# Layer norm between the last two attentions of a two-block model, with tokens on partitions

## The chip, the core and the metric

The kernel runs on one core of a Trainium2 chip, in one launch. The metric is the device time in microseconds of one execution. Three runs of the kernel before took 1597.56, 1601.13 and 1601.93 us; the median, 1601.13 us, is its time.

## The reference

The model is a block with a convolution, a dilated window attention and a feed-forward part, followed by a second block of two layers. In the second block each layer is an attention (first one with selected keys, then one with stick-breaking weights), an output projection, a residual and a layer norm. The change touches the layer norm of the first of these two layers, whose result is the input of the second layer's projections.

```python
D_MODEL, SEQ, N_HEADS = 1024, 512, 16
LN_EPS = 1e-5
ALPHA = (2.0 * DEPTH_2) ** 0.25

def layer_norm(x, g, b):
    xf = x.astype(jnp.float32)
    mu = jnp.mean(xf, axis=-1, keepdims=True)
    var = jnp.mean(jnp.square(xf - mu), axis=-1, keepdims=True)
    return ((xf - mu) * lax.rsqrt(var + LN_EPS) * g + b).astype(x.dtype)

def stick_breaking_mixer(x, w_in, w_out):
    q, k, v, g = jnp.split(x @ w_in, 4, axis=-1)
    ...
    return (o * jax.nn.silu(g)) @ w_out

def second_block(x, ...):
    for i in range(DEPTH_2):
        ...                                   # y = attention of layer i
        x = layer_norm(ALPHA * x + y, ln_g[i], ln_b[i])
    return x
```

## The kernel before

All activations lie turned: channels on the 128 partitions, the 512 tokens along the row, so that 1024 channels are 8 blocks of 128x512. A matrix product takes both operands in two parts, a rounded high part and the rest (`Ah`, `Al` of an activation, `whi`, `wlo` of a weight), and adds three matmuls for each of 8 chunks of the contraction (lines 301 to 303): high by high, low by high, high by low.

Weights come in blocks of 512 KB. SyncE's queue loads the raw block (line 87, two buffers), ScalarE rounds it to `whi` (line 119, four buffers), and GpSimd subtracts to get `wlo` (line 123, four pieces of 128x256). A block's raw buffer is free for the next load when GpSimd is through with it, its `whi` buffer when TensorE is.

TensorE runs in the order in which the program is written: a stream of (product, chunk) pairs is pulled, and small pieces of work are put behind a given number of further chunks (`pe.after`). The other engines' orders are laid out by a scheduler from the program's order and readiness.

The stage of the change starts when the attention of the layer is through. `Outward` holds the output projection's 8 products. Of blocks 0 to 3 all chunks but the last have been run before; `run` (line 1213 on) runs those last chunks, then blocks 4 and 5 over all 512 tokens, then blocks 6 and 7 for the first 256 tokens (the first half) and then for the second. `done` (line 1209) adds each block to the residual `e` (the tiles named S) and calls `summed`.

`Between` is the norm in question. Its sums go over channels, that is over partitions, so it makes them on TensorE with matrices of ones. After block 3 it takes half of the channels' mean as a middle (`middle`, line 1237) and subtracts it from every block (line 1249), squares on ScalarE (1252, 1255) and adds squares and values on GpSimd and VectorE (1257 to 1260). For each half `stats` (line 1275) sends the sums, rounded and rest, through four matmuls with ones, takes Ln and Exp for the scale, and goes over all 8 blocks: subtract the mean (1296), multiply by gain and scale (1297), high part on ScalarE (1298), low part on VectorE (1299). `normed` then runs the first three of the next layer's 8 gate products in halves, chunk by chunk for all three together, as the chunks of `Ah` and `Al` appear.

`Last` is the norm at the end of the program. It turns each block with transposes on TensorE (line 1312), copies it to a tile `y` with tokens on partitions, takes statistics along the row on VectorE (1319, 1341), and Ln and Exp for the scales of two row tiles at a time (line 192 is the helper that issues them).

Behind the stage follow the gates' Tanh on ScalarE, the first query and key products of the next layer (lines 530 to 560), and GpSimd's additions of the next residual (line 1204). These stand in a loop over head pairs that lasts to about 1545 us.

Of the kernel before, what the change touches and what calls it, by code (L numbers as in the profile page):

```python
# [10 lines left out]
F32 = mybir.dt.float32  # L11
# [39 lines left out]
STATS = (9, 14)  # L51
# [97 lines left out]
def model_kernel(ctx: ExitStack, tc: tile.TileContext, x, norm1_g, w_in, gate_b, conv_w, conv_b, conv_norm_g,  # L149
# [27 lines left out]
    def f32(t):  # L177
        return t.bitcast(F32)
# [40 lines left out]
    ones_h = const.tile([128, 128], F32R, name="ones_h")  # L219
# [203 lines left out]
    with tc.tile_pool(name="rows", bufs=1) as rows, tc.manual_schedule(engines={  # L423
# [19 lines left out]
        nc.vector.tensor_scalar(ones_h, zero128, 2.0 / D, None, op0=OP.add)  # L443
# [774 lines left out]
    class Between(Outward):  # L1218

        def summed(self, c, ts):
            part = self.part
            if c == 1:
                nc.vector.tensor_add(part, self.es[0], self.es[1])
            elif c in (2, 3):
                nc.vector.tensor_add(part, part, self.es[c])
            if c == 3:
                h, l = act_pair(self.pool, "st", 2)
                nc.scalar.copy(h, part)  # L1230
                nc.vector.tensor_sub(l, part, f32(h))
                pe.after(4, lambda: self.middle(h, l))
            self.ready.append((c, ts))
            if self.centred:
                self.shift(c, ts)

        def middle(self, h, l):
            pm = ps_t()
            nc.tensor.matmul(pm, ones_h, h, start=True, stop=False)
            nc.tensor.matmul(pm, ones_h, l, start=False, stop=True)  # L1240
            nc.scalar.copy(self.mid, pm)
            self.centred = True
            for a in self.ready:
                self.shift(*a)

        def shift(self, c, ts):
            t = slice(*ts)
            es, s1, s2 = [e[:, t] for e in self.es], self.s1[:, t], self.s2[:, t]
            nc.vector.tensor_sub(es[c], es[c], self.mid[:, t])
            eng = nc.gpsimd if c < 4 else nc.vector  # L1250
            if c == 0:
                nc.scalar.activation(s2, es[c], AF.Square)
            else:
                sq = self.pool.tile([128, S], F32, name="sq", bufs=3)[:, t]
                nc.scalar.activation(sq, es[c], AF.Square)
                if c == 5:
                    eng.tensor_add(s1, es[4], es[5])
                elif c > 5:
                    eng.tensor_add(s1, s1, es[c])
                eng.tensor_add(s2, s2, sq)  # L1260
            if c == ND - 1:
                half = TS.index(ts)
                pe.after(STATS[half], lambda: self.stats(half))

        def normed(self, pool, ys, prods):

            self.pool, self.ready, self.centred, self.ys = pool, [], False, ys
            self.mid, self.part, self.s1, self.s2, self.var = (pool.tile([128, S], F32, name=n)
                                                               for n in ("mid", "part", "s1", "s2", "var"))
            self.run()  # L1270
            for half in range(2):
                pe.together(*[p[half] for p in prods])
            pe.finish()

        def stats(self, half):
            t = slice(*TS[half])
            n = S // 2
            p1, p2 = ps_t()[:, :n], ps_t()[:, :n]
            for p, s in ((p1, self.s1), (p2, self.s2)):
                h, l = (a[:, :n] for a in act_pair(self.pool, "st", 2))  # L1280
                nc.scalar.copy(h, s[:, t])
                nc.vector.tensor_sub(l, s[:, t], f32(h))
# [303 lines left out]
```

## Time and profile before

| | |
|---|---|
| median of three runs | 1601.13 us |
| the profiled execution | 1601.03 us |
| its span, first to last instruction | 1598.9 us |
| TensorE busy | 1527.2 us, 96% of the span |
| VectorE, ScalarE, GpSimd busy | 70%, 53%, 50% |
| mean granted clock of TensorE | 0.98 |

A page of a profile gives for each engine the time in which it was busy, in a picture of 40 slices and as groups of instructions by line. PE is TensorE, DVE VectorE, ACT ScalarE, POOL GpSimd, SP SyncE. PEclk is the clock that TensorE was granted as a share of 2.4 GHz: 1.00 is 2.4 and 0.50 is 1.2 GHz, the two levels. A row of the timeline begins with the start and the length of an instruction; what stands in brackets is the idle time of its engine just before it and what ended that.

### The profile page before, as it was taken

To read this page: it belongs to the slowest core of one execution; us is meant where nothing else is said; L and a number is where in the kernel's file an instruction comes from. 1 tells how busy PE (TensorE), PEld (TensorE's weight loads), DVE (VectorE), ACT (ScalarE), POOL (GpSimd) and SP (SyncE) were. 2 spreads that over 40 slices of the span, in tenths; PEclk is the share of its full clock that TensorE was granted. 3 is DMA by queue.
4 is the path that set the end of the run, shared out by engine and by line. 5 is a ranking of instruction groups with operands and counts; after the bars stand their busy time and mean duration, and the time that the engine had idled before them with its cause. 6 is when DMAs were issued, how large, how long until landed. Compare 5 with 4: busy or idle time off the path is not lost.

```text
span 1598.9 us, 21378 instructions
## 1 busy us (share of the span) xinstructions
PE 1527.2 (96%) x7870; PEld 1296.7 (81%) x7870; DVE 1121.4 (70%) x1837; ACT 845.4 (53%) x1524; POOL 806.5 (50%) x680
## 2 busy tenths in 40 slices
PE   7999799998999999999999999999999789999996
PEld 6877688887878888888888887888887678888885
DVE  8998777776166467727735669988887765777764
ACT  4455787777552444424333444366766345666652
POOL 3789944332744653454444474445442875334324
PEclk9999899999999999999999999999999899999998
DMA  4323212221233423343333242322220313212212
GB/s 149 88 87 98 86 54 73 60 67 40 67 105 105 126 86 92 93 118 91 90 110 89 84 125 66 80 80 66 67 67 14 92 40 106 67 54 80 67 52 80
DMA packets 234604, 130.37 MB, mean 82 GB/s; under 512 B 5206, under 2 KB 232774, under 8 KB 234500
## 3 DMA queue, kind: packets, MB, share of 16 engines
q1 hardware_dynamic: 234356, 128.75, 27.7%
q8 instruction: 62, 1.02, 0.3%
q14 instruction: 42, 0.34, 0.1%
q10 hardware_dynamic: 144, 0.26, 0.0%
HBM read 126.90 MB, written 2.10 MB: 81 GB/s over the span
## 4 chain that ended last, share of the span: by engine, by line
PE 57%; DVE 23%; ACT 7%; POOL 5%; issue 5%; DMA 2%; DVEq 0%; SPq 0%; ACTq 0%; POOLq 0%
PE pj L301 10%; PE pj L302 9%; PE pj L303 9%; PE s L302 5%; PE s L303 5%; PE s L301 5%; DVE pt L831 5%; PE o L512 2%; POOL wlo L123 2%; PE pt L593 2%; PE pj L325 2%; PE pj L327 2%; PE pj L326 2%; POOL S L837 2%; DVE score L1442 1%
## 5 line engine op out<-in xcount | busy, mean ns | idle before, releaser
L123 POOL TENSOR_TENSOR wlo<-wraw,whi 128x256 fp32r<-128x256 f32 (+2 forms) x548 | 653.8, 1218 | 684.4 <-ACT whi L119 639.0
L301 PE MATMUL pj<-Ah,whi 128*128 128x512 f32 (+3 forms) x896 | 362.2, 404 | 15.2 <-DVE v L718 9.8
L119 ACT CAST whi<-wraw 128x1024 fp32r<-128x1024 f32 (+3 forms) x255 | 243.8, 965 | 224.3 <-PE pj L302 82.1
L303 PE MATMUL pj<-Ah,wlo 128*128 128x512 f32 (+3 forms) x896 | 350.4, 391 | 2.5 <-POOL wlo L123 2.5
L302 PE MATMUL pj<-Al,whi 128*128 128x512 f32 (+3 forms) x896 | 350.7, 391 | 0.0
L301 PEld LDWEIGHTS pj<-Ah,whi 128*128 128x128 f32 (+1 forms) x896 | 171.2, 191 | 41.9 <-issue 9.1
L303 PEld LDWEIGHTS pj<-Ah,wlo 128*128 128x128 f32 (+1 forms) x896 | 170.3, 190 | 39.1 <-POOL wlo L123 3.4
L302 PEld LDWEIGHTS pj<-Al,whi 128*128 128x128 f32 (+1 forms) x896 | 171.1, 191 | 24.4
L301 PE MATMUL s<-Ah,whi 128*128 128x512 f32 (+1 forms) x352 | 135.8, 386 | 4.0 <-ACT Ah L1298 4.0
L302 PE MATMUL s<-Al,whi 128*128 128x512 f32 (+1 forms) x352 | 135.7, 386 | 3.6 <-DVE Al L1299 3.6
L303 PE MATMUL s<-Ah,wlo 128*128 128x512 f32 (+1 forms) x352 | 135.6, 385 | 1.0 <-POOL wlo L123 1.0
L831 DVE SCALAR_TENSOR_TENSOR pt<-S,cw,pt 128x496 f32<-128x496 f32 (+19 forms) x180 | 124.8, 738 | 6.4 <-ACT pt L824 3.8
L325 PE MATMUL pj<-whi,Ah 128*128 128x256 f32 x384 | 112.4, 293 | 1.4 <-DVE q L533 1.4
L596 DVE TENSOR_TENSOR PTl<-pt,PTh 128x512 fp32r<-128x512 f32 x144 | 86.0, 598 | 32.9 <-ACT PTh L595 31.9
L327 PE MATMUL pj<-whi,Al 128*128 128x256 f32 x384 | 108.4, 282 | 0.0
L326 PE MATMUL pj<-wlo,Ah 128*128 128x256 f32 x384 | 108.3, 282 | 0.0
L192 ACT ACTIVATE P<-P,nm 128x128 f32<-128x128 f32 (+3 forms) x128 | 72.0, 563 | 63.2 <-DVE nm L626 61.9
L744 DVE SCALAR_TENSOR_TENSOR u<-ur,fw,u 128x511 f32<-128x511 f32 x44 | 74.9, 1705 | 37.5 <-ACT u L743 37.5
L837 POOL TENSOR_TENSOR S<-S,o 128x511 f32<-128x511 f32 (+29 forms) x60 | 78.2, 1317 | 15.4 <-ACT o L836 14.3
L595 ACT CAST PTh<-pt 128x512 fp32r<-128x512 f32 x144 | 73.1, 513 | 19.6 <-PE pt L593 19.1
L302 PEld LDWEIGHTS s<-Al,whi 128*128 128x128 f32 x352 | 67.8, 193 | 17.1 <-DVE Al L1299 4.5
L301 PEld LDWEIGHTS s<-Ah,whi 128*128 128x128 f32 x352 | 67.9, 193 | 17.1 <-ACT Ah L1298 4.6
(334 smaller groups left out, 3250.8 us busy)
## 6 DMA issues: line engine op xcount, KB each, us to landing
wraw<-in_w_in_dram SPq DMA_DIRECT2D x56, 512.0 KB
wraw<-in_w_up_dram SPq DMA_DIRECT2D x44, 512.0 KB
wraw<-in_w_in_a_dram SPq DMA_DIRECT2D x36, 512.0 KB
wraw<-in_w_in_b_dram SPq DMA_DIRECT2D x32, 512.0 KB
wraw<-in_w_down_dram SPq DMA_DIRECT2D x16, 512.0 KB
wraw<-in_w_attn_out_dram SPq DMA_DIRECT2D x8, 512.0 KB
wraw<-in_w_conv_out_dram SPq DMA_DIRECT2D x8, 512.0 KB
wraw<-in_w_out_dram SPq DMA_DIRECT2D x8, 512.0 KB
```

What stands on the lines that cost most here:

```text
L119: nc.scalar.copy(h, s)
L123: nc.gpsimd.tensor_sub(l[:, k], s[:, k], h[:, k].bitcast(F32))
L301: nc.tensor.matmul(o, hv[:, k, :], ah, start=first, stop=False)
L302: nc.tensor.matmul(o, hv[:, k, :], al, start=False, stop=False)
L303: nc.tensor.matmul(o, lv[:, k, :], ah, start=False, stop=last)
L325: nc.tensor.matmul(o, ah, hv, start=k == 0, stop=False)
L326: nc.tensor.matmul(o, ah, lv, start=False, stop=False)
L327: nc.tensor.matmul(o, al, hv, start=False, stop=k == 7)
L596: nc.vector.tensor_sub(l[:, :at], pt[:, :at], f32(h)[:, :at])
L744: nc.vector.scalar_tensor_tensor(u[:, 1:], v[:, :S - 1], fw[:, 1, j:j + 1], u[:, 1:], op0=OP.mult, op1=OP.add)
L831: nc.vector.scalar_tensor_tensor(o, a, w, o, op0=OP.mult, op1=OP.add)
L837: nc.gpsimd.tensor_add(o, o, t)
```

## The change

`Between` now works as `Last` does up to the scales. Their common part is the new class `Turned`: each block is turned as soon as it is complete, copied to `y`, and its statistics are taken along rows (`bn_stats`, `bn_aggr`). When a half's last block is turned, `finish` takes the scales of the half's two row tiles, and the mean times the scale, negative (`off`, 128x1). Then the two row tiles of the half are normalised in place, 512 columns at a time, one on VectorE, the other on ScalarE. `back` turns the result again: for each of the 8 blocks two transposes into one PSUM bank, ScalarE's high part with gain and bias per partition, the full value `e` (on ScalarE for odd blocks, on VectorE for even ones), and VectorE's subtraction for the low part. The backs stand 7, 9, 11, ... chunks behind the turning of block 7 (`BACK`). The middle, the squares and the matmuls with ones go, and with them the matrix `ones_h`. `Last` is the same as before, apart from where its lines stand.

```diff
-STATS = (9, 14)
+BACK = (7, 2)
...
-    class Between(Outward):
-        def summed(self, c, ts):
...
-        def middle(self, h, l):
...
-        def shift(self, c, ts):
...
-        def stats(self, half):
...
-    class Last(Outward):
+    class Turned(Outward):
         SPANS = {3: (0, 4), 6: (4, 7), 7: (7, 8)}
         def summed(self, c, ts):
...
             pe.after(4, turn)
+        def buffers(self, pool):
...
+        def scales(self, ts):
+            rstd = self.rstd[:, ts[0]:ts[-1] + 1]
+            for t in ts:
+                nc.vector.bn_aggr(self.mv[:, t], self.stats[:, t])
+            act(rstd, self.mv[:, ts[0]:ts[-1] + 1, 1], AF.Ln, bias=eps5)
+            act(rstd, rstd, AF.Exp, scale=-0.5)
+
+    class Between(Turned):
+        def normed(self, pool, ys, prods):
+            self.buffers(pool)
+            self.off = pool.tile([128, NT], F32, name="off")
+            self.ys = ys
+            self.run()
+            for half in range(2):
+                pe.together(*[p[half] for p in prods])
+            pe.finish()
+
+        def finish(self, ts):
+            self.scales(ts)
+            mv, rstd, off = self.mv, self.rstd, self.off
+            for t in ts:
+                nc.vector.scalar_tensor_tensor(off[:, t:t + 1], mv[:, t, 0:1], -1.0, rstd[:, t:t + 1], op0=OP.mult, op1=OP.mult)
+            for k in range(0, D, 512):
+                for t in ts:
+                    z = self.y[:, t, k:k + 512]
+                    if t % 2:
+                        nc.scalar.activation(z, z, AF.Identity, bias=off[:, t:t + 1], scale=rstd[:, t:t + 1])
+                    else:
+                        nc.vector.tensor_scalar(z, z, mv[:, t, 0:1], rstd[:, t:t + 1], op0=OP.subtract, op1=OP.mult)
+            for c in range(ND):
+                pe.after(BACK[0] + BACK[1] * c, lambda c=c: self.back(c, ts))
+
+        def back(self, c, ts):
+            if ts[0] == 0:
+                self.ys.append(act_pair(keep, "A", ND))
+            pt = ps_t()[:, :S // 2]
+            for i, t in enumerate(ts):
+                nc.tensor.transpose(pt[:, 128 * i:128 * i + 128], self.y[:, t, 128 * c:128 * c + 128], ident)
+            h, l = (a[:, 128 * ts[0]:128 * ts[-1] + 128] for a in self.ys[c])
+            g, b = lng[:, c:c + 1], lnb[:, c:c + 1]
+            e = self.pool.tile([128, S // 2], F32, name="e", bufs=3)
+            nc.scalar.activation(h, pt, AF.Identity, bias=b, scale=g)
+            if c % 2:
+                nc.scalar.activation(e, pt, AF.Identity, bias=b, scale=g)
+            else:
+                nc.vector.tensor_scalar(e, pt, g, b, op0=OP.mult, op1=OP.add)
+            nc.vector.tensor_sub(l, e, f32(h))
+
+    class Last(Turned):
```

On TensorE, where block 7 of the second half (`pj`, over `ogh` and `ogl`, the attention's output) has run its first chunks, before: the four matmuls with ones for the first half's statistics.

```order
L303 MATMUL pj_11393<-ogh_9329,wlo_11243 128x256
L1283 MATMUL pt_11397<-sth_11399,ones_d_72 128x256
L1284 MATMUL pt_11397<-stl_11400,ones_d_72 128x256
L1283 MATMUL pt_11398<-sth_11405,ones_d_72 128x256
L1284 MATMUL pt_11398<-stl_11406,ones_d_72 128x256
L301 MATMUL pj_11393<-ogh_9612,whi_11242 128x256
L302 MATMUL pj_11393<-ogl_9613,whi_11242 128x256
```

And at the place that answers to it, with the change:

```order
L301 MATMUL pj_11404<-ogl_9914,whi_11239 128x256
L302 MATMUL pj_11404<-ogh_9913,wlo_11240 128x256
L1287 MATMUL pt_11416<-ident_69,y_11155 128x128 x2
L300 MATMUL pj_11404<-ogh_10196,whi_11239 128x256
L301 MATMUL pj_11404<-ogl_10197,whi_11239 128x256
L302 MATMUL pj_11404<-ogh_10196,wlo_11240 128x256
L1227 MATMUL pt_11426<-ident_69,S8_10876 128x128 x2
L300 MATMUL pj_11404<-ogh_10499,whi_11239 128x256
```

The matmuls with ones are gone; in their place two transposes of the normalised `y` (L1287) and, a chunk later, the turning of block 6's second half (L1227) stand between the chunks. Line numbers are those of the changed file.

On ScalarE, from the first half's sums on, before (`sth` the rounded sums, `Ah` the high parts, `whi<-wraw` a weight cast):

```order
L1281 CAST sth_11399<-s1_11159 128x256
L1281 CAST sth_11405<-s2_11160 128x256
L119 CAST whi_11491<-wraw_11289 128x1024
L1286 ACTIVATE var_11161<-pt_11397 128x256
L1255 ACTIVATE sq_11389<-S8_10878 128x256
L192 ACTIVATE var_11161<-var_11161,eps5_71 128x256
L192 ACTIVATE var_11161<-var_11161 128x256
L119 CAST whi_11504<-wraw_11329 128x1024
L1298 ACTIVATE Ah_11416<-S8_10686,vec_77 128x256
L1298 ACTIVATE Ah_11422<-S8_10716,vec_77 128x256
```

And from the last copy of the first half on, with the change:

```order
L1228 COPY y_11155<-pt_11375 128x2x128
L192 ACTIVATE rstd_11158<-mv_11157,eps5_71 128x2
L119 CAST whi_11463<-wraw_11287 128x1024
L192 ACTIVATE rstd_11158<-rstd_11158 128x2
L1276 ACTIVATE y_11155<-y_11155,off_11159,rstd_11158 128x512 x2
L1291 ACTIVATE Ah_11414<-pt_11416,vec_76 128x256
L1228 COPY y_11155<-pt_11426 128x2x128
L1291 ACTIVATE Ah_11435<-pt_11437,vec_76 128x256
L1293 ACTIVATE e_11440<-pt_11437,vec_76 128x256
L1291 ACTIVATE Ah_11450<-pt_11452,vec_76 128x256
L119 CAST whi_11485<-wraw_11328 128x1024
```

A weight cast now stands between Ln and Exp of the scales (L192), and the high parts (L1291) and full values (L1293) come from PSUM in turn with the copy of block 6's second half (L1228) and another cast.

## Rows read from the trace of the kernel before

**Rows 1.** Windows: stretch, length, busy us per engine (count), clock, DMA share, GB/s.

```profile
1236.70:1305.90 69.20, 54.49 (x311) 48.60 (x310) 56.37 (x81) 26.52 (x47) 53.24 (x56) 0.85 0.21 61
1245.10:1249.20 4.10, 4.10 (x13) 3.19 (x12) 1.59 (x2) 1.53 (x2) 2.91 (x5) 0.58 0.51 152
1293.30:1296.80 3.50, 3.50 (x17) 3.50 (x18) 3.50 (x4) 0.38 (x2) 3.50 (x3) 0.51 0.02 5
1306.00:1545.00 239.00, 236.60 (x1399) 207.35 (x1398) 165.11 (x258) 151.44 (x303) 103.44 (x130) 1.00 0.25 71
1318.40:1323.00 4.60, 4.59 (x38) 4.60 (x39) 1.13 (x2) 3.60 (x6) 3.04 (x5) 1.00 0.43 118
1559.70:1580.85 21.15, 20.52 (x133) 18.20 (x132) 5.87 (x11) 5.79 (x9) 9.62 (x14) 1.00 0.17 51
```

**Rows 2.** TensorE's waits from 1236.7 to 1305.9: us, times, longest.

```profile
PE pt L1283 <- ACT sth L1281: 5.1, 2, 4.7
...
PE s L301 <- ACT Ah L1298: 4.0, 3, 2.3
...
PE s L302 <- DVE Al L1299: 3.6, 4, 1.5
```

**Rows 3.** Groups by line and shape, 1236 to 1306 us: busy, mean ns, idle.

```profile
L123 POOL TENSOR_TENSOR wlo<-wraw,whi 128x256 fp32r<-128x256 f32 x32 | 30.0, 970 | 8.7 <-ACT whi L119 8.7
...
L1297 DVE SCALAR_TENSOR_TENSOR S<-S,vec,var 128x256 f32<-128x256 f32 x16 | 13.9, 916 | 0.0
```

**Rows 4.** Groups by line and shape, the whole run.

```profile
L743 ACT ACTIVATE u<-ur,fw 128x512 f32<-128x512 f32 x44 | 35.8, 815 | 17.0 <-DVE ur L741 17.0
...
L718 DVE TENSOR_TENSOR v<-pj,v 128x256 fp32r<-128x256 f32 x48 | 20.1, 418 | 12.7 <-ACT v L717 12.5
...
L1157 ACT ACTIVATE ogh<-tmp 128x512 fp32r<-128x512 f32 x16 | 10.1, 632 | 15.0 <-DVE tmp L1155 11.2 <-DVE tmp L1478 3.8
...
L1313 ACT COPY y<-pt 128x256 f32<-128x256 f32 x4 | 1.5, 367 | 7.3 <-PE pt L1312 7.3
```

**Rows 5.** Timeline of TensorE inside the stage: start, length, instruction.

```profile
1257.77 0.28 PE L301 MATMUL s<-ogh,whi 128*128 128x256 f32 x1
...
1260.65 0.28 PE L301 MATMUL pj<-ogh,whi 128*128 128x256 f32 x1
...
1292.13 0.39 PE L301 MATMUL s<-Ah,whi 128*128 128x256 f32 x1 [1.28 <-ACT Ah L1298]
...
1293.24 0.47 PE L302 MATMUL s<-Al,whi 128*128 128x256 f32 x1 [0.73 <-DVE Al L1299]
```

**Rows 6.** Timeline of TensorE and ScalarE in the last norm.

```profile
1556.26 0.39 PE L301 MATMUL pj<-ogh,whi 128*128 128x512 f32 x1
...
1569.78 0.63 PE L1312 MATMUL pt<-ident,e 128*128 128x128 f32 x4 [0.63 <-DVE e L1209]
...
1580.84 0.38 PE L1312 MATMUL pt<-ident,e 128*128 128x128 f32 x2
...
1580.98 0.37 PE L301 MATMUL pj<-ogh,whi 128*128 128x256 f32 x1
...
1581.18 0.29 PE L302 MATMUL pj<-ogl,whi 128*128 128x256 f32 x1
...
1582.46 0.30 ACT L192 ACTIVATE rstd<-mv,eps 128x2 f32<-128x2 f32 x1 [0.83 <-DVE mv L1341]
...
1582.79 0.20 ACT L192 ACTIVATE rstd<-rstd 128x2 f32<-128x2 f32 x1
...
1589.18 0.81 ACT L1352 ACTIVATE y<-y,mr,nr 128x512 f32<-128x512 f32 x1
```

**Rows 7.** Timeline of GpSimd, ScalarE and TensorE just behind the stage.

```profile
1305.65 2.53 POOL L1204 TENSOR_TENSOR e<-Ah,Al 128x512 f32<-128x512 f32 x2
...
1314.69 1.05 ACT L119 CAST whi<-wraw 128x1024 fp32r<-128x1024 f32 x1 [3.08 <-DMA wraw<-in_w_in_b_dram]
...
1318.41 0.36 PE L325 MATMUL pj<-whi,Ah 128*128 128x256 f32 x1 [1.44 <-DVE q L533]
```

More of the change, by code (lines that the diff above doesn't have):

```diff
@@ L218, in model_kernel @@
     ones_d = const.tile([128, 128], F32R, name="ones_d")
-    ones_h = const.tile([128, 128], F32R, name="ones_h")
     ones_b = const.tile([128, 128], F32R, name="ones_b")
@@ L442, in model_kernel @@
         nc.vector.tensor_scalar(ones_d, zero128, 1.0 / D, None, op0=OP.add)
-        nc.vector.tensor_scalar(ones_h, zero128, 2.0 / D, None, op0=OP.add)
         nc.vector.tensor_scalar(ones_b, zero128, 0.0, None, op0=OP.add)
@@ L1216, in run @@
                 pe.skewed(p)
-    class Between(Outward):
-        def summed(self, c, ts):
[L1223 to L1235, printed above, removed]
-        def middle(self, h, l):
[L1238 to L1244, printed above, removed]
-        def shift(self, c, ts):
[L1247 to L1273, printed above, removed]
-        def stats(self, half):
[L1276 to L1282, printed above, removed]
-                nc.tensor.matmul(p, ones_d, h, start=True, stop=False)
-                nc.tensor.matmul(p, ones_d, l, start=False, stop=True)
-            mu, var = self.part[:, t], self.var[:, t]
-            nc.scalar.activation(var, p1, AF.Square)
-            nc.vector.tensor_copy(mu, p1)
-            nc.vector.tensor_sub(var, p2, var)
-            act(var, var, AF.Ln, bias=eps5)
-            act(var, var, AF.Exp, scale=-0.5)
-            for c, e in enumerate(self.es):
-                e, g, b = e[:, t], lng[:, c:c + 1], lnb[:, c:c + 1]
-                if half == 0:
-                    self.ys.append(act_pair(keep, "A", ND))
-                h, l = (a[:, t] for a in self.ys[c])
-                (nc.gpsimd if c > 2 else nc.vector).tensor_sub(e, e, mu)
-                nc.vector.scalar_tensor_tensor(e, e, g, var, op0=OP.mult, op1=OP.mult)
-                nc.scalar.activation(h, e, AF.Identity, bias=b)
-                nc.vector.scalar_tensor_tensor(l, e, b, f32(h), op0=OP.add, op1=OP.subtract)
@@ L1323, in summed @@
             pe.after(4, turn)
-        def normed(self, pool):
+        def buffers(self, pool):
             self.pool = pool
@@ L1331, in normed @@
+    class Last(Turned):
+        def normed(self, pool):
+            self.buffers(pool)
             self.g, self.b = (pool.tile([128, D], F32, name=n) for n in "gb")
@@ L1337, in finish @@
         def finish(self, ts):
-            mv, g, b = self.mv, self.g, self.b
-            rstd = self.rstd[:, ts[0]:ts[-1] + 1]
-            for t in ts:
-                nc.vector.bn_aggr(mv[:, t], self.stats[:, t])
-            act(rstd, mv[:, ts[0]:ts[-1] + 1, 1], AF.Ln, bias=eps5)
-            act(rstd, rstd, AF.Exp, scale=-0.5)
-            rstd = self.rstd
+            self.scales(ts)
+            mv, rstd, g, b = self.mv, self.rstd, self.g, self.b
             for t in ts:
```

## The prediction

> **What bounds the kernel now.** I read first the windows, because an average over the whole span hides the one stage that the change touches. The reader is to see two things in them [rows 1]. The stretch behind the stage (1306 to 1545 us) has TensorE busy for 236.6 of 239 us at the full clock: there a microsecond won or lost earlier is simply moved along. The stage itself, from the first last-chunk matmul of the output projection (1236.70) to the first full-width matmul of the next layer (1305.90), takes 69.2 us, with TensorE busy 54.5 of them at a mean clock of 0.85, while VectorE is busy for 56.4.
>
> Second, the waits of TensorE inside the stage [rows 2]: the three longest groups sum to 5.1 + 4.0 + 3.6 = 12.7 us. All are waits for numbers of the norm: the rounded sums that go into the matmuls with ones, the high parts (Ah), the low parts (Al).
>
> Third, what the engine that it waits for is doing: VectorE's steps at L1297 take 0.916 us on average for 256 columns [rows 3], against 0.418 us for a two-operand step of the same width with one operand in PSUM [rows 4]. GpSimd's subtractions for the weights, in the same stage, take 0.970 us [rows 3].
>
> Fourth, the clock. There are four stretches in the stage at the level of 1.2 GHz; the first (from 1245.1) and the last (from 1293.3) stand in [rows 1]. Each follows waits, the last one waits of 1.28 and 0.73 us [rows 5]. It costs 3.5 x 0.49 = 1.7 us, the first 4.1 x 0.42 = 1.7, four of them some 7 us. So about 20 of the 69 us are waits and what they do to the clock.
>
> **What goes, what comes, and what it costs.** The statistics by matmuls with ones go, with the middle, the squares, the sums, and the passes of VectorE and GpSimd over eight blocks in each half. What comes is the mechanism that the last norm uses already, up to the scales; then two normalising steps of 512 columns for each row tile, 16 pairs of transposes back, and for each block and half one high part, one full value and one low part.
>
> *From the start of the stage to the turning of block 7, first half.* TensorE's order here becomes that of the last norm, instruction for instruction, so I take its time from there: 1556.26 to 1580.84 is 24.6 us [rows 6], which includes a wait of 0.63 us for VectorE at 1569.78. ScalarE has two weight casts more here than there (the first two gate blocks), each waiting for its DMA. They stand ahead of two copies of turned blocks that nothing needs for microseconds; I count them at nothing, and at 1.05 us each [rows 7] if that slack is gone.
>
> *From there to the end, TensorE's own work.* A matmul of 256 columns starts every 0.12 us (24 of them from 1257.77 to 1260.65 [rows 5]), so a group of three takes 0.36. There are 12 groups left of the projection and 48 of the gates: 21.6 us. A pair of transposes takes 0.14 us and delays the start after the next matmul by 0.08 (1580.84, 1580.98, 1581.18 [rows 6]): 0.22. One pair closes the first half, two come from the second half, 16 are the way back: 19 x 0.22 = 4.2 us. Sum 25.8 us.
>
> *Its waits there.* The first pair back stands 0.22 + 7 x 0.36 = 2.7 us behind the turning of block 7. The chain of the scales: Ln ends 1.92 us after that turning [rows 6]; then a weight cast of 1.05 us [rows 7] stands on ScalarE between Ln and Exp; Exp takes 0.20 [rows 6]; two 128x1 steps on VectorE, not seen before, I take at 0.3 together, the Ln's time for as small a tile [rows 6] (between 0, if something hid them, and 0.84, two steps of 256 columns [rows 4]); a normalising step of 512 columns on ScalarE, 0.81 us [rows 6]. That ends at 4.3: a wait of 1.6 us, behind which the last five groups of the projection and the turning of block 6's second half are queued. Then the first block's Ah and Al take their round trip beside those five groups, and I allow 0.4 us for the first Al.
>
> In the second half ScalarE has a queue ahead of the scales: two evacuations in hand, a copy of 0.37, five evacuations, Ln, Exp and the 0.81. An evacuation of 256 columns from PSUM with a bias and a scale per partition does not occur before; its bounds are the plain copy, 0.37 [rows 4], and 0.81, twice the columns with both. I take 0.367 + (0.815 - 0.632) = 0.55, the difference being that of 512 columns with and without the two per-partition operands [rows 4]. Together 5.5 us, against 7 groups and 4 pairs, 3.4 us, on TensorE: 2.1 us of wait, with the gates of the first half from their fourth chunk on queued behind it. After that the gates find everything ready, since a pair back comes every 2 groups and a chunk of the three gates takes 3. Waits together 4.1 us; bounds 0.6 (the first without its cast, the second hidden) and 8.2 (twice as long).
>
> *The clock.* A wait of 1.44 us at 1318.41 [rows 7] left it at 1.00 [rows 1]; 1.28 and 0.73 us close together before 1293.3 did not [rows 5]. My two waits lie around that. I take one low stretch, 1.7 us; bounds none and three.
>
> *VectorE's low parts.* Al is a subtraction of two SBUF tiles while GpSimd may be working on weights. I take 0.42 us, the undisturbed row [rows 4], since GpSimd has weights to do for only part of the stage; the other end is 0.92 [rows 3]. Sixteen times the difference is 8 us on an engine with room beside TensorE's 30, so some 2 us at most reach the end. The Trainium skill (SBUF — State Buffer, section Who interferes with whom) says that a VectorE instruction with two SBUF inputs contends with a GpSimd instruction that reads SBUF, and that one fully blocks the other; by that rule the change keeps 16 such instructions and the sum would be up to 2 us longer. The trace agrees with it: 0.916 against 0.418 us.
>
> *Sum.* New stage 24.6 + 25.8 + 4.1 + 1.7 = 56.2 us, against 69.2: 13.0 us less. GpSimd loses its subtractions and sums for the norm, so its eight additions for the last residual no longer run past the end of the stage: before, they ended at 1308.18, and only then came the next weights, whose successor's DMA ScalarE waited for (3.08 us) and TensorE behind it (1.44 us) [rows 7]. I count 1.2 us of that 1.44 as won, bounds 0 and 1.4. The order of the loads on SP is the same. Total 14.2 us.
>
> The profiled execution took 1601.03 us (a span of 1598.9 and 2.1 around it), next to the median of 1601.13; 1601.0 - 14.2 = 1586.8.
>
> **The rivals.**
> 1. *ScalarE's queue becomes the bound.* Casts that wait for DMA stand in its order between the scales and the evacuations. If the raw block is late by 3.08 us [rows 7] at two of them, 6 us more reach TensorE: 1593. For it: such waits occur before. Against it: the change takes away most of the VectorE steps beside which GpSimd ran slow, so the loads that wait for GpSimd start earlier.
> 2. *The clock stays low from the first wait to the end of the gates.* At the low level a matmul of 256 columns takes 3.5/17 = 0.206 us [rows 1], so 60 groups cost 60 x 3 x 0.086 = 15.5 us more, less the 1.7 counted: 1600.6, no change. For it: two waits and many transposes between short matmuls. Against it: 26 transposes among matmuls ran at 1.00 in the last norm (1559.7 to 1580.85 [rows 1]). The Trainium skill (TensorE: Matmul & The Clock Gate, section Part 4: PE-mode transpose) says that the full clock does not engage for transposes; by that rule this rival would be the likelier, and the trace speaks against its mattering among matmuls.
> 3. *The weights take the gain back.* If the next stage were led by its DMAs, it would wait out the 14 us: 1601. Against it: a DMA share of 0.25 from 1306 to 1545 and TensorE busy for 99% [rows 1].
> 4. *The round trips don't overlap; slower.* Each of the 16 pairs back is followed by 0.38 us of transposes, up to two evacuations of 0.55 and a subtraction of up to 0.92 before the block can be used. If TensorE waited out these 2.4 us at each, that is 38 us in place of the 4.1 counted: 1621. It is slower from 14.2/16 = 0.9 us for each block upwards. Against it: three PSUM banks for turned blocks, two groups between a pair and the next, three between the uses.
>
> **How the numbers follow.** The forecast, 1587 with its own range of 1581 to 1592, has 0.80; rival 1 0.10; rival 2 0.04; rival 3 0.03; rival 4 0.03. A measurement of this kernel can tell about 0.3%, 4.8 us, from no change. Forecast and rival 1 lie below 1596: 0.90 faster. Rivals 2 and 3 make 0.07 for the same, rival 4 0.03 for slower. The range runs from 1580 (no low clock, no wait but the 0.63 us: 14.2 + 1.7 + 4.1 and 0.2 of the queries' wait, rounded) to 1595, past rival 1.
>
> **What would show it.** In the new profile the stretch from the projection's last chunks to the first full-width matmul of the next layer should last 53 to 61 us, TensorE's waits in it sum to 3 to 9 us, with one of 1 to 2.5 us at the first pair back of each half, and at most two low stretches of the clock. VectorE should be busy for about half of it. The 1.44 us wait on the queries behind it should shrink. I am wrong if the stage is over 64 us, if waits of 1 us or more stand at single blocks inside the gates, or if the stage is short and the end is not earlier.

## The result: 1584.0 us in place of 1601.5, and the profile after

| | before | after |
|---|---|---|
| median of runs | 1601.51 us (4 runs, 1597.56 to 1601.93) | 1584.03 us (4 runs, 1582.43 to 1587.29) |
| ratio | | 0.9899, 95% interval 0.9877 to 0.9921 |
| profiled execution, span | 1601.03, 1598.9 us | 1583.91, 1582.1 us |

Predicted were 1586.8 us. A second comparison (after_again, below) gave 0.9909, 0.9897 to 0.9922: by the two medians the change is worth some 14 to 17 us.

Windows of the kernel after, columns as in [rows 1]: the stage, its two parts (up to and from the turning of block 7's first half), the two stretches behind the first wait, the time around the second wait, and what answers to the long stretch behind the stage.

```profile
1233.08:1288.90 55.82, 52.06 (x366) 48.31 (x365) 30.82 (x58) 28.90 (x51) 35.13 (x44) 0.97 0.26 76
1233.08:1257.66 24.58, 23.97 (x147) 20.99 (x146) 8.36 (x14) 9.68 (x13) 16.88 (x24) 1.00 0.38 109
1257.66:1288.90 31.24, 28.09 (x221) 27.32 (x220) 22.46 (x44) 19.22 (x38) 18.25 (x20) 0.95 0.17 50
1262.50:1264.00 1.50, 1.50 (x10) 1.50 (x11) 1.14 (x2) 1.38 (x3) 1.28 (x2) 0.73 0.00 0
1264.00:1267.50 3.50, 3.50 (x22) 3.50 (x21) 2.31 (x7) 2.12 (x5) 0.00 (x0) 0.63 0.54 150
1272.40:1276.00 3.60, 2.42 (x19) 2.24 (x20) 2.65 (x8) 3.40 (x8) 0.00 (x0) 1.00 0.48 150
1288.90:1528.00 239.10, 237.34 (x1401) 207.82 (x1400) 165.59 (x258) 151.99 (x303) 102.42 (x129) 1.00 0.25 71
```

The stage went from 69.20 to 55.82 us, and VectorE's work in it from 56.4 to 30.8 us [rows 1]. The clock is low in one stretch: 1.5 x 0.27 + 3.5 x 0.37 = 1.7 us.

TensorE's waits in the stage (us in total, times, longest), against 14.6 us in eleven waits before, the longest of them in [rows 2]:

```profile
PE pt L1287 <- ACT y L1276: 1.9, 1, 1.9
PE pt L1287 <- DVE y L1278: 1.1, 1, 1.1
PE pt L1227 <- DVE S L1207: 0.6, 1, 0.6
```

The timeline of ScalarE, VectorE and TensorE between the first half's scales and the first pair back, and TensorE at the second half's first pair:

```profile
1259.29 0.30 ACT L192 ACTIVATE rstd<-mv,eps 128x2 f32<-128x2 f32 x1 [0.83 <-DVE mv L1250]
1259.52 1.05 ACT L119 CAST whi<-wraw 128x1024 fp32r<-128x1024 f32 x1
1260.47 0.20 ACT L192 ACTIVATE rstd<-rstd 128x2 f32<-128x2 f32 x1
...
1260.70 0.75 DVE L1271 SCALAR_TENSOR_TENSOR off<-mv,rstd 128x1 f32<-128x1 f32 x2 [0.77 <-ACT rstd L192]
...
1262.47 0.41 PE L1287 MATMUL pt<-ident,y 128*128 128x128 f32 x2 [1.93 <-ACT y L1276]
...
1273.46 0.78 PE L1287 MATMUL pt<-ident,y 128*128 128x128 f32 x2 [1.08 <-DVE y L1278]
```

The cast stands between Ln and Exp as the order said, and the wait behind it is 1.93 us.

Behind the stage, the rows that answer to [rows 7]:

```profile
1296.67 1.05 ACT L119 CAST whi<-wraw 128x1024 fp32r<-128x1024 f32 x1 [2.07 <-DMA wraw<-in_w_in_b_dram]
...
1300.38 0.35 PE L324 MATMUL pj<-whi,Ah 128*128 128x256 f32 x1 [0.42 <-DVE q L531]
```

The queries' wait fell from 1.44 to 0.42 us, but from the stage's end to the span's end it is 293.2 us, against 293.0. The rest of the difference lies ahead of the stage, which began at 1233.08 us in place of 1236.70 with the same instructions ahead of it. So the 16.8 us between the two spans are 13.4 in the stage, 3.6 ahead of it and -0.2 behind; the other 0.3 of the 17.1 us between the two profiled executions lie outside the spans.

### The profile page after: what moved, and what is told of

Same layout as the page of the kernel before. It is cut to its first block, busy times and chain, and to the rows that moved or that the text cites. A ratio compares the mean times of both kernels' runs of the same rounds, so it can differ in the third digit from the quotient of the medians.

```text
span 1582.1 us, 21462 instructions
## 1 busy us (share of the span) xinstructions
PE 1521.4 (96%) x7924; PEld 1294.3 (82%) x7924; DVE 1095.5 (69%) x1813; ACT 847.9 (54%) x1528; POOL 787.2 (50%) x667
## 4 chain that ended last, share of the span: by engine, by line
PE 59%; DVE 21%; ACT 8%; issue 5%; POOL 4%; DMA 2%; DVEq 0%; SPq 0%; ACTq 0%; POOLq 0%
PE pj L300 10%; PE pj L301 10%; PE pj L302 10%; PE s L300 5%; PE s L301 5%; PE s L302 5%; DVE pt L829 5%; PE o L510 3%; PE pt L591 2%; POOL wlo L123 2%; PE pj L324 2%; PE pj L326 2%; PE pj L325 2%; POOL S L835 2%; ACT whi L119 1%
## 5 line engine op out<-in xcount | busy, mean ns | idle before, releaser
L123 POOL TENSOR_TENSOR wlo<-wraw,whi 128x256 fp32r<-128x256 f32 (+2 forms) x548 | 646.9, 1205 | 688.9 <-ACT whi L119 645.8
L302 PE MATMUL pj<-Ah,wlo 128*128 128x512 f32 (+3 forms) x896 | 349.4, 390 | 2.9 <-POOL wlo L123 2.9
L301 PE MATMUL pj<-Al,whi 128*128 128x512 f32 (+3 forms) x896 | 349.5, 390 | 0.0
L302 PEld LDWEIGHTS pj<-Ah,wlo 128*128 128x128 f32 (+1 forms) x896 | 169.3, 189 | 39.9 <-POOL wlo L123 4.2
L301 PEld LDWEIGHTS pj<-Al,whi 128*128 128x128 f32 (+1 forms) x896 | 170.3, 190 | 24.2
L302 PE MATMUL s<-Ah,wlo 128*128 128x512 f32 (+1 forms) x352 | 134.2, 381 | 1.0 <-POOL wlo L123 1.0
L301 PE MATMUL s<-Al,whi 128*128 128x512 f32 (+1 forms) x352 | 134.2, 381 | 0.0
L192 ACT ACTIVATE P<-P,nm 128x128 f32<-128x128 f32 (+3 forms) x128 | 72.1, 563 | 63.3 <-DVE nm L624 62.0
L591 PE MATMUL pt<-ident,P 128*128 128x128 f32 x480 | 76.7, 273 | 2.4 <-ACT P L192 0.9
L302 PEld LDWEIGHTS s<-Ah,wlo 128*128 128x128 f32 x352 | 66.6, 189 | 14.1 <-POOL wlo L123 1.4
```

The lines of the kernel that those rows point to most:

```text
L123: nc.gpsimd.tensor_sub(l[:, k], s[:, k], h[:, k].bitcast(F32))
L301: nc.tensor.matmul(o, hv[:, k, :], al, start=False, stop=False)
L302: nc.tensor.matmul(o, lv[:, k, :], ah, start=False, stop=last)
L591: nc.tensor.transpose(pt[:, at:at + 128], self.P[r][:, k0:k0 + 128], ident)
```

## The experiments

A group is the three matmuls of one chunk, a pair is the two transposes of one block back (L1287 in the kernel after). Stage lengths are taken in each kernel's one profile, from the first last-chunk matmul of the projection to the first full-width matmul of the next layer; ratios are to the kernel before on the same chip. The kernels after and after_again had stages of 55.82 and 55.95 us, and before 69.20, fill_gates 69.38: the length repeats to some 0.2 us, the start of the stage does not.

**after_again.** The kernel after, unchanged.

> The changed kernel once more, for its ratio to the kernel before on the chip of its neighbours here, and for another profile of what lies ahead of the stage. Theory (the 17 us are the stage's own 13.4 and chance ahead of it, since the stage began at 1232.6 to 1236.7 us in ten profiles of either kind, with the same instructions ahead of it): a ratio of 0.990 to 0.992, 1584 to 1588. Rival (the change makes the stretch ahead of the stage 3.6 us shorter): the stage begins before 1233.5 us again and the ratio is 0.989 or less.

1585.98 us (4 runs), 0.9909, 0.9897 to 0.9922; the stage began at 1235.23. Over all profiles the five kernels made from before began it at 1233.61 to 1236.70, mean 1235.2, the nine made from after at 1232.61 to 1237.44, mean 1234.8. The theory held. The two kinds begin the stage at the same times, so the 3.6 us ahead of it are chance; what the profiles show of the change itself is the stage's 13.4.

**fill_before, fill_gates.** Matmuls that nothing reads, inside waits of the kernel before:

```
 def fill(self, n):
     o = ps_o()
     for _ in range(n):
         nc.tensor.matmul(o[:, :S // 2], ident_r, self.src[0][:, :S // 2], start=True, stop=True)
 ...
+if k == 0 and self.fill: self.fill(0)      # 19, second half 10
 nc.tensor.matmul(o, hv[:, k, :], ah, start=first, stop=False)
+if k == 0 and self.fill: self.fill(1)      # 12, second half 6
 nc.tensor.matmul(o, hv[:, k, :], al, start=False, stop=False)
```

> The kernel before, with matmuls of 256 columns that nothing reads inside its seven longest waits of the stage: 16 ahead of the middle's matmuls, 40 and 4 ahead of the sums of each half, 19 and 12, and 10 and 6, ahead of the first Ah and Al of the gates of each half. It separates the waits from the low clock behind them. Theory (of the 69.2 us some 15 are waits and some 7 the low clock): the four low stretches go and the stage is 4 to 7 us shorter, since part of a low stretch lies ahead of another wait that then grows; 1594.5 to 1597.5. Rival (VectorE and GpSimd contend and alone set the stage's length, so that the clock costs nothing): all of it comes back as longer waits, within 1 us of 1601.5.

1601.87 us, 1.0012 (1.0003 to 1.0021), stage 72.6 us. It decides nothing: with the matmuls in the code, two weight casts in place of one came between the rounding of the sum and the copy of the middle on ScalarE, and VectorE waited 6.6 us for that copy in place of 2.9. fill_gates leaves out the ones that did this.

> The kernel before, with matmuls that nothing reads in the waits of the gates alone: 19 and 12 ahead of the first Ah and Al of the first half, 4 ahead of the second half's sums, 10 and 6 ahead of its first Ah and Al. The order on the other engines stays that of before, which fill_before had not kept. Theory (low clock is a cost of its own): the stretches at 1278.4 to 1283.2 and 1293.3 to 1296.8 go, 2.4 + 1.7 us of them, of which some lies ahead of other waits that then grow: 1 to 4 us shorter, 1597.5 to 1600.5. Rival (the low clock lies beside VectorE's passes, which set the end of the stage): the waits behind grow by what the clock gives back, 1601.5 within 0.7.

1600.98 us, 1.0004 (0.9995 to 1.0012), stage 69.38 us. Windows of fill_gates: the stretch in which the clock is still low, around the wait for the first half's sums, and the places of two low stretches of before:

```profile
1263.30:1273.50 10.20, 5.96 (x26) 5.77 (x27) 9.82 (x19) 4.30 (x10) 6.70 (x9) 0.50 0.34 97
...
1277.10:1282.00 4.90, 4.19 (x36) 3.99 (x35) 4.90 (x9) 1.42 (x3) 3.28 (x4) 1.00 0.09 18
...
1291.10:1295.50 4.40, 4.36 (x33) 4.01 (x33) 4.40 (x7) 0.98 (x3) 3.29 (x3) 1.00 0.00 0
```

The kernel before at the first and the second of these, for the third see [rows 1]:

```profile
1266.10:1272.90 6.80, 4.17 (x18) 3.99 (x19) 6.50 (x15) 3.20 (x7) 3.29 (x5) 0.50 0.28 80
1278.30:1283.20 4.90, 4.87 (x23) 4.88 (x24) 4.90 (x8) 1.42 (x3) 3.17 (x4) 0.50 0.10 23
```

Two rows of its timeline, and the same two places of the kernel before:

```profile
1267.55 0.58 PE L1295 MATMUL pt<-sth,ones_d 128*128 128x256 f32 x1 [6.35 <-ACT sth L1293]
...
1302.72 0.39 PE L305 MATMUL s<-Al,whi 128*128 128x256 f32 x1 [0.88 <-DVE Al L1311]
```

```profile
1268.73 0.58 PE L1283 MATMUL pt<-sth,ones_d 128*128 128x256 f32 x1 [4.68 <-ACT sth L1281]
...
1303.78 0.38 PE L302 MATMUL s<-Al,whi 128*128 128x256 f32 x1 [0.88 <-DVE Al L1299]
```

At the last two places the clock is up where it was down (1.00 against 0.50 and 0.51), and in this profile it is up in the stretch behind the first waits too. The fourth stretch, around the wait for the sums, stayed low, for 10.2 us in place of 6.8. Yet the waits end 32.07 and 67.24 us behind the start of the stage, against 32.03 and 67.08. What the clock gave TensorE went into the waits (6.35 for 4.68). The rival was right: the stage of before is as long as the chain on the other engines, and the low clock of those three stretches costs nothing of its own; of the fourth these runs don't tell. VectorE's busy column says so too: 4.90 of 4.90 and 4.40 of 4.40 us in the two windows at full clock.

**before_on_vector, before_less.** GpSimd's share of the norm given to VectorE, and the subtraction of the mean left out:

```
-(nc.gpsimd if c > 2 else nc.vector).tensor_sub(e, e, mu)
+nc.vector.tensor_sub(e, e, mu)            # before_on_vector; before_less: no line
...
-eng = nc.gpsimd if c < 4 else nc.vector   # before_on_vector alone
+eng = nc.vector
```

> The kernel before, with GpSimd's subtractions and sums of the norm (3 of 512 and 10 of 256 columns) given to VectorE. Theory (TensorE waits for the number of passes over all channels, whoever does them): VectorE gets some 3 x 0.69 + 10 x 0.42 = 6.3 us more work in the stage and runs less slowed, 0.42 in place of 0.92 us for the 11 steps that GpSimd's stood beside, 5.5 us less; weights are still subtracted on GpSimd beside it, so that half of the slowing stays: 0 to 4 us slower, 1601 to 1605. Rival (the contention of the two engines is what the change removed): VectorE's steps fall to 0.42 us, the stage gets 4 us or more shorter, under 1597.5.

1596.95 us (12 runs), 0.9978 (0.9968 to 0.9987), stage 66.56. Faster, though VectorE does 13 steps more. The groups of its norm, busy us and mean ns, where before had 916 in [rows 3]:

```profile
L1297 DVE SCALAR_TENSOR_TENSOR S<-S,vec,var 128x256 f32<-128x256 f32 x16 | 10.7, 700 | 0.0
...
L1296 DVE TENSOR_TENSOR S<-S,part 128x256 f32<-128x256 f32 x16 | 8.9, 596 | 0.0
```

The theory, 0 to 4 us slower, missed. The rival, 4 us or more shorter, was nearer: the ratio is worth 3.5 us and the stage loses 2.6, but a step at L1297 takes 0.70 us, half way from the 0.92 of before to the rival's 0.42. So the two engines' slowing of each other is a part of what the change removed, and not the whole: 66.6 us is far from 55.8. How much of the 2.6 us is the quicker steps and how much the hand-overs from GpSimd to VectorE that went with them, this run does not separate.

> The kernel before without the subtraction of the mean from the blocks, 6 on VectorE and 10 on GpSimd; its output leaves that out. TensorE, ScalarE and their order are untouched. Theory as it stands after fill_gates and before_on_vector (the stage of before is as long as VectorE's passes, with GpSimd's beside them, and neither TensorE's clock nor its own work counts there): 6 steps of 0.42 us go and the slowed ones speed up as in before_on_vector, 2.5 + 3 us and some waits for GpSimd: 1593 to 1596. Rival (the round trips through the sums, TensorE and ScalarE set it): within 2 us of 1600.5.

1597.62 us, 0.9979 (0.9968 to 0.9989), stage 65.15, 4.1 us less; the ratio is worth 3.4 us, where 4.5 to 7.5 were expected. The direction is the theory's, the size falls short of it. Taking away passes over the channels shortens the stage, with TensorE untouched; but VectorE was busy for only 49.3 of its 65.2 us. That the rest is round trips between the engines is an argument, not shown.

**cast_behind, third_cast.** Both order weight casts on ScalarE behind its normalising steps. cast_behind moves the last cast issued ahead of the scales, which is the second gate block's, not the third's as its expectation says; the third's and the fourth's then come later too. third_cast moves the third's:

```
+if t == 1 and k:   # the second normalising step of the first half
+    W.hold = lambda cast, z_=z_: tc.add_manual_dep(cast, z_.ins.name, no_sync)
...
+self.cast = nc.scalar.copy(h, s).ins; self.hold and self.hold(self.cast)   # at each cast emitted behind it
```

> The changed kernel, with the third gate block's weight cast ordered behind the first normalising step of ScalarE, so that it no longer stands between Ln and Exp of the first half. Theory (the chain of the scales sets TensorE's wait at the first pair back, 1.93 us): the wait falls by about 0.95, the cast's time there, to 1.0 us, the stage from 55.8 to some 54.9 us, and to 53.3 if the low stretch of the clock behind the wait (1.6 us) goes with it; 1581.5 to 1583.1 us. Rival (the weights are the next thing late, since the cast comes 3 us later): TensorE waits at a gate's first chunk in its place, no change, 1584.

1589.82 us (5 runs), 0.9928 (0.9915 to 0.994), stage 59.35: 3.5 us longer than after. That is slower than theory and rival had it. The first wait did go, to 0.15 us, and no low clock followed. But ScalarE's timeline, TensorE's in the second half, and the window behind it have:

```profile
1272.57 1.04 ACT L119 CAST whi<-wraw 128x1024 fp32r<-128x1024 f32 x1 [1.96 <-DMA wraw<-in_w_in_b_dram]
...
1274.56 0.41 PE L1289 MATMUL pt<-ident,y 128*128 128x128 f32 x2 [1.74 <-DVE mv L1250]
...
1277.35 0.83 PE L1289 MATMUL pt<-ident,y 128*128 128x128 f32 x2 [1.67 <-DVE y L1280]
```

```profile
1276.00:1283.00 7.00, 5.66 (x27) 5.48 (x28) 4.59 (x12) 4.02 (x8) 3.21 (x3) 0.51 0.26 77
```

A cast that comes later sets its raw block free later; the next block but one then landed late, and its cast stood in ScalarE's order ahead of the second half's copies and scales. Two waits, 3.4 us, stand there in place of one of 1.08, and a low stretch of the clock that begins between them is worth 5.66 x 0.49 = 2.8 us. This is the prediction's first rival, made to happen by a cast that was put off.

> The changed kernel, with only the cast that stands between Ln and Exp (that of the third gate block, at 1259.52 us) ordered behind the second normalising step of ScalarE; the two casts ahead of it keep their place, unlike in cast_behind. Theory (in cast_behind the chain of the scales did get short, a wait of 0.2 us and no low clock in place of 1.93 and 1.6, and what was lost came from a block cast later, whose successor's transfer ended 1.96 us late and stood in ScalarE's order ahead of the second half's scales): with the early casts kept the loss is gone and the gain of the first half stays, 1.7 + 1.6 us, less some 0.5 for the third gate's low parts: a stage of 53.0 us, 1581.2. Rival (any cast put off makes the second half late): the second half's waits are 3 us or more again, 1584 to 1590.

1585.51 us (4 runs), 0.9907 (0.9892 to 0.9921), stage 55.47. The first wait and its low clock are gone, 3.6 us, and the stage is only 0.4 us shorter. TensorE at the second half's first pair, and the window behind it:

```profile
1274.49 0.78 PE L1289 MATMUL pt<-ident,y 128*128 128x128 f32 x2 [1.67 <-DVE y L1280]
```

```profile
1275.00:1280.00 5.00, 5.00 (x30) 5.00 (x31) 3.09 (x5) 2.97 (x6) 2.41 (x2) 0.66 0.22 74
```

Both expectations missed: the stage is 2.5 us longer than the theory's, and the waits are not the rival's 3 us. No cast waited for its weights ahead of the second half's scales; TensorE simply came to the second half's pairs earlier than the second half's scales, which pass through the same busy VectorE and ScalarE queues. The wait grew by 0.6 us, to 1.67, and now has a low stretch behind it, 5.0 x 0.34 = 1.7 us. That is 2.3 of the 3.6 us; 0.4 is what the stage gained, and the rest went into smaller pauses, 0.2 us of it near the start of the stage, where the wait of 0.6 us was 0.8.

**late_second, late_and_third.** The second half's pairs 5 groups later; and with third_cast's edit. The first changes nothing but TensorE's order:

```
-pe.after(BACK[0] + BACK[1] * c, lambda c=c: self.back(c, ts))
+pe.after(BACK[0] + LATER * (ts[0] // 2) + BACK[1] * c, lambda c=c: self.back(c, ts))   # LATER = 5
```

> The changed kernel with the second half's pairs back asked for 12 groups behind the turning of block 7 in place of 7; the order on the other engines stays. Theory (TensorE can do gates of the first half, which are ready, while the second half's scales are computed): the second wait, 1.08 us, goes, stage 54.7 us, 1583. Rival (the evacuations of the second half, now in 5 groups less time, are late for the gates): waits on Ah or Al of 1 us or more, 1584 to 1587.

1587.06 us (4 runs), 0.9911 (0.9897 to 0.9926). The stage is the theory's, the time isn't: the second wait is gone, the stage 54.47 us, with no wait over 0.2 us in its gates; but its end comes 294.4 us ahead of the span's end, 1.2 more than after. GpSimd's last addition and TensorE's wait for the queries show where:

```profile
1293.53 1.29 POOL L1202 TENSOR_TENSOR e<-Ah,Al 128x512 f32<-128x512 f32 x1
...
1304.99 0.36 PE L324 MATMUL pj<-whi,Ah 128*128 128x256 f32 x1 [2.02 <-DVE q L531]
```

The additions need the second half's low parts, which now come later. They end 2.9 us behind the stage, in place of 1.2 in the kernel after, the weights behind them come later, and the queries wait 2.02 us in place of 0.42.

> Both edits: the third gate block's cast behind the second normalising step, and the second half's pairs 5 groups later. Theory (in third_cast what the first wait gave back went into the second wait, 1.67 us, and the low clock behind it, about 1.7 us): both waits are covered, the clock stays up, stage 52 us, 1580.5 to 1582. Rival (a third thing, the weights of the third gate or the evacuations, is late in turn): no better than third_cast, 1584 to 1586.

1584.13 us (4 runs, 1581.51 to 1586.4), 0.9896 (0.9882 to 0.991). The stage is as the theory had it, the median time is the rival's; two executions took under 1582 us, two over 1586. The stage's window, and behind it the rows that answer to [rows 7]:

```profile
1233.51:1285.48 51.97, 50.75 (x365) 46.79 (x364) 30.17 (x58) 28.54 (x51) 33.52 (x40) 1.00 0.28 82
```

```profile
1287.28 1.29 POOL L1202 TENSOR_TENSOR e<-Ah,Al 128x512 f32<-128x512 f32 x1
...
1294.96 1.05 ACT L119 CAST whi<-wraw 128x1024 fp32r<-128x1024 f32 x1 [3.77 <-DMA wraw<-in_w_in_b_dram]
...
1298.67 0.36 PE L324 MATMUL pj<-whi,Ah 128*128 128x256 f32 x1 [2.12 <-DVE q L531]
```

As in late_second, GpSimd's additions run far past the stage's end, 3.1 us (1287.28 + 1.29 against 1285.48), the next weights come behind them, and the queries wait 2.12 us. In third_cast, where the pairs were not later, they run 0.3 us past it. So it is the later pairs that cost this, and of a stage 4.0 us shorter 1.0 is given back. What is left, 3 us, the times don't tell from the kernel after: 0.9896 against 0.9909 on the same chip, with intervals that overlap. Its profiled execution, 1581.51, also began the stage 1.7 us earlier than after_again's.

**back_early.** `BACK = (3, 2)` in place of `(7, 2)`.

> The changed kernel with the pairs back asked for 3 groups behind the turning of block 7 in place of 7 (both halves); Exp then follows Ln directly in ScalarE's order in the first half. Theory (the chain of scales sets the moment at which the first pair can start, about 4.7 us behind the turning): TensorE comes 4 x 0.36 = 1.44 us earlier, the chain ends about 0.95 earlier, so the wait is 1.93 + 1.44 - 0.95 = 2.4 us in the first half and about 1.08 + 1.4 = 2.5 in the second, each with a low stretch; the groups jumped over are done behind the pairs, so that what is lost is the growth of the waits, 0.5 + 1.4, and one more low stretch of 1.6: 1586 to 1588. Rival (the pairs' round trip to the gates is what is late): earlier pairs help, 1582 to 1583.

1588.45 us (5 runs), 0.9922 (0.9908 to 0.9935), stage 58.04: 2.2 us longer than after. TensorE's timeline:

```profile
1264.46 0.69 PE L1287 MATMUL pt<-ident,y 128*128 128x128 f32 x2 [1.57 <-DVE y L1278]
...
1276.64 0.83 PE L1287 MATMUL pt<-ident,y 128*128 128x128 f32 x2 [3.05 <-DVE y L1278]
```

As the theory had it in sum (4.6 us against 4.9), each is a wait as long as the chain of the scales lasts beyond TensorE's work; the first is shorter by 0.8 than expected, since VectorE's steps were quicker there (the two normalising steps 1.00 us, against 1.82 in the kernel after); the second is longer. A low stretch stands behind the second alone: the first, 1.57 us, left the clock at 1.00.

**fill_after.** 16 and 9 such matmuls ahead of the first pairs of each half of the kernel after.

> The changed kernel, with 16 matmuls of 256 columns that nothing reads issued by TensorE ahead of the first pair back, and 9 ahead of the first pair of the second half: 1.9 and 1.1 us of work inside waits of 1.93 and 1.08. Theory (the low clock behind the first wait is what the idle engine costs, 1.6 us): the pairs start when they did, the low stretch at 1263 to 1266 is gone, the stage is 54.2 us and the time 1582.4. Rival (the clock falls because of the transposes and short matmuls around it): the low stretch stays, 55.8 us and 1584, or some tenths more where the matmuls overrun the wait.

1585.62 us (5 runs), 0.9908 (0.9895 to 0.992). The low stretch is gone, the clock 1.00 in all of the stage, which is 54.60 us, 1.2 shorter than after. In the time nothing of it shows: in the profiled execution 3.4 us more lie behind the stage, in the last norm, where a weight block landed late (ScalarE's cast waited 4.27 us for it, 2.66 in the kernel after) and TensorE waited 2.5 us, with a low stretch behind that:

```profile
1552.75 0.96 PE L1227 MATMUL pt<-ident,e 128*128 128x128 f32 x4 [2.46 <-DVE e L1207]
```

One profile can't tell whether that is chance. That the idle engine, and not the transposes, brought the clock down at the first pair is shown by the stage: same transposes, wait filled, clock 1.00.

**pairs_twice.** Each pair of transposes back issued twice.

```
-for i, t in enumerate(ts):
+for i, t in 2 * list(enumerate(ts)):
```

> The changed kernel, with every pair of transposes back issued twice into the same bank: 16 pairs more. Theory (inside the gates TensorE is the bound and a pair costs its engine time, 0.14 to 0.22 us): the stage is 2.2 to 3.5 us longer, 1586.2 to 1587.5. Rival (the way back is bound by ScalarE's and VectorE's evacuations, with room on TensorE): less than 1 us, 1584 to 1585.

1586.25 us (4 runs), 0.9911 (0.9898 to 0.9924): as a ratio not to be told from after_again's 0.9909. The stage is 57.70 us, 1.9 longer than after, a little less than the theory's 2.2. TensorE's rows in the gates, in the kernel after with one pair and here with two:

```profile
1269.06 0.28 PE L302 MATMUL s<-Ah,wlo 128*128 128x256 f32 x1
1269.18 0.38 PE L1287 MATMUL pt<-ident,y 128*128 128x128 f32 x2
1269.31 0.37 PE L300 MATMUL pj<-Ah,whi 128*128 128x256 f32 x1
1269.52 0.28 PE L301 MATMUL pj<-Al,whi 128*128 128x256 f32 x1
```

```profile
1279.24 0.28 PE L302 MATMUL pj<-Ah,wlo 128*128 128x256 f32 x1
1279.36 0.60 PE L1287 MATMUL pt<-ident,y 128*128 128x128 f32 x4
1279.71 0.36 PE L300 MATMUL s<-Ah,whi 128*128 128x256 f32 x1
1279.92 0.28 PE L301 MATMUL s<-Al,whi 128*128 128x256 f32 x1
```

From L302 to L301 it is 0.46 us with one pair and 0.68 with two, where 0.24 is two matmuls: 0.22 us a pair, 3.5 for 16. What did not lengthen the stage, 1.6 us, is the second wait (1.08 us), which is gone, and some half a microsecond of smaller pauses. The edit also moved the second half's Ln and Exp forward in ScalarE's order, which has a share in that. TensorE is the bound in the gates, as the theory had it, with small pauses left.

## Why the prediction was right, point by point

- **From the start to the turning of block 7.** 24.58 us against 24.6: the order of the last norm gave the time of the same order here, and the two weight casts more cost nothing.
- **TensorE's own work from there.** 31.24 us less the waits of 3.0 and the low clock of 1.7 is 26.5, against 25.8. A pair costs the 0.22 us taken, by the rows at pairs_twice. So the 0.7 lies in pauses that the sum did not have; 0.4 of it is in the second half's first pair, whose second transpose waited for ScalarE's step (0.78 us in place of 0.38).
- **The first wait.** 1.93 against 1.6 us, with the cast where it was put. The two 128x1 steps took 0.75 us, not 0.3 (0.23 in the second half). third_cast shows that the cast is the cause: without it the wait is gone, not only 0.95 us shorter, because GpSimd's subtractions, which follow the cast, no longer ran beside VectorE's steps (0.23 and 1.00 us there, in place of 0.75 and 1.82).
- **The other waits.** Nothing at the first Al (0.4 taken) and 1.08 us in the second half (2.1 taken): ScalarE's queue ahead of the second half's scales was shorter than counted, and at Ln it idled for 0.49 us until VectorE had the aggregates. An evacuation took 0.561 us on average, against 0.55.
- **The clock.** One stretch, 1.7 us, at the first wait, as predicted; the number one was a choice between none and three, not worked out.
- **VectorE's low parts.** 0.776 us on average, nearer to the end that was not taken (0.92) than to 0.42; hidden all the same: VectorE is busy for 30.8 of 55.8 us, and no wait at an Al stands in the gates. Of the rule in the Trainium skill (SBUF — State Buffer, section Who interferes with whom) these runs bear out that the two engines slow each other: 0.92 against 0.70 us for the step of [rows 3] with GpSimd's share taken away.
- **Sum of the stage.** 55.82 against 56.2 us. The mechanism is the predicted one, the closeness is in part luck: 0.7 us too little for TensorE's own work stands against 1.1 too much for the waits. The profiled execution's 1583.9 against 1586.8 us is a matter of where the stage began.
- **Behind the stage.** This term is the one that failed. The additions on GpSimd still run past the end of the stage, by 1.2 us in place of 2.3:

```profile
1288.86 1.28 POOL L1202 TENSOR_TENSOR e<-Ah,Al 128x512 f32<-128x512 f32 x1
```

  The queries' wait shrank by 1.0, close to the 1.2 counted, and yet nothing of it reached the end. Later waits took it back in small pieces, at the last norm among them (0.84 against 0.63 us). It should have been counted at nothing.
- **The account of the kernel before failed too**, though not in the sum: "So about 20 of the 69 us are waits and what they do to the clock". fill_gates shows that the clock's share was not a cost there, as far as it reaches: with it up in three of the four stretches the stage was as long. The low clock lay beside a chain on VectorE and its neighbours that ended when it ended. Since the new stage was added up from its own instructions and not by taking costs off the old one, the error did not enter the time.
- **The rivals.** The first did not happen, but is real: cast_behind brought it about with one cast, at 3.5 us in the stage. The second (a clock that stays low among transposes): late_and_third ran the whole stage, 32 transposes back included, at 1.00. The rule of the Trainium skill (TensorE: Matmul & The Clock Gate, section Part 4: PE-mode transpose) that was weighed there doesn't hold for transposes among matmuls in these runs. The third showed only where the second half's pairs came later (late_second and late_and_third), at 1.2 and 1.0 us. The fourth: no waits of 1 us at single blocks in the gates.

## What to carry to other kernels

Add up the new stage from its own instructions and the order they stand in; taking supposed costs off the old stage would have counted a low clock that, where it was tried, cost nothing, since it lay beside a longer chain. Before a low clock or a wait is called a cost, fill it with work that nobody reads and see whether the next wait ends earlier. And where one wait is removed, ask at once which chain is second: here nearly all that was won at the first wait came back at the second half's scales, and a quarter of what both edits together won came back at the next stage's weights.

## What the runs showed of the hardware that was not expected

- With the same instructions ahead of it (but for one that fills the matrix no longer needed), the stage began anywhere from 1232.6 to 1237.4 us in fourteen profiles, while its own length repeats to 0.2. A single profile's difference from another of 4 us says nothing until it is located.
- Behind the same waits of 1.32 and 0.62 us, with the same instructions, the clock fell to 0.58 in the profile of before [rows 1] and stayed at 1.00 in that of fill_gates; the stage was as long.
- The chain of the scales itself is slowed by GpSimd. VectorE's steps after the first half's Exp in the kernel after, where GpSimd's subtractions ran beside them, and in back_early, where GpSimd was idle until 1266.95:

```profile
1260.64 3.14 POOL L123 TENSOR_TENSOR wlo<-wraw,whi 128x256 fp32r<-128x256 f32 x4 [4.41 <-ACT whi L119]
...
1261.37 1.82 DVE L1278 TENSOR_SCALAR y<-y,mv,rstd 128x512 f32<-128x512 f32 x2
```

```profile
1263.63 0.23 DVE L1271 SCALAR_TENSOR_TENSOR off<-mv,rstd 128x1 f32<-128x1 f32 x2 [0.60 <-ACT rstd L192]
1263.77 1.00 DVE L1278 TENSOR_SCALAR y<-y,mv,rstd 128x512 f32<-128x512 f32 x2
```

  A 128x1 step took 0.12 us alone and 0.37 beside GpSimd, a normalising step with one input tile 0.50 and 0.91. The Trainium skill (SBUF — State Buffer, section Who interferes with whom) counts `tensor_scalar` among the operations that can take the pair of ports that VectorE shares with GpSimd; the trace agrees in that the normalising step, a `tensor_scalar`, is the slower beside GpSimd, 0.91 against 0.50 us. The prediction had weighed that section's rule at Al alone.
